# A decoder layer whose gates and branches swap the stationary and the moving operand, and whose second FFN sums its norm two units later

## The chip, the cores and the metric

One core of one Trainium2 chip runs the whole layer in one launch. The metric is the device time of the launch in microseconds (us); the median of three runs of the kernel before is 2172.03 us (2171.75 to 2172.18).

## What is computed

The layer works on T = 272 tokens (16 meta tokens, which the output drops, and 256 others) of width 2048, in float32:

```
h += 1/2 * SwiGLU_1(RMSNorm(h))
u  = RMSNorm(h);  z = u @ W_in      # q, k, v, q_idx, k_idx, w_idx, x_c, B, C, gate_attn, gate_conv
y_A = sparse attention over the top 64 keys
y_B = B * conv3_causal(C * x_c)
merged = sigmoid(gate_conv) * (y_B @ W_conv_branch) + sigmoid(gate_attn) * (y_A @ W_attn_branch)
h += merged @ W_out
h += 1/2 * SwiGLU_2(RMSNorm(h))
```

The change lies in the lines of `merged`, in the order of `merged @ W_out`, and at the start of SwiGLU_2. Gates have 2048 rows of weights, branches 1024 each, `W_out` 2048; all three have 2048 columns.

## The kernel before, in words

**Products.** Each float32 operand is split into a high and a low float32r part, and a product is the sum of three: high times high, high times low, low times high. Weights come from memory in chunks of 1 MB (128 x 2048), issued by SP (L94). A chunk is split in two *units* of 128 x 1024: ScalarE copies the high part (`whi`, L109), VectorE subtracts it (`wlo`, L110). `Stream.next` hands out the blocks of a unit one after the other. When it begins a unit it issues, in this order: what is due `early`, one of the `steps`, the split of the unit that is three units ahead (AHEAD = 3, four buffers), and then what is due `later`. A function filed with lag n, once a product's last unit has been taken, is issued with the n-th unit that begins from then on. Each engine keeps that order, so that what is due `later` stands behind the split on VectorE and ScalarE.

**Three forms of product.** `mac` (L265 to L267, used by `fmajor`) holds a weight block of 128 x 128 and moves the activations, 272 columns at a time, three matmuls a block. `paired` (L279, L280) also holds the weight block, and moves the high and the low part of 256 tokens side by side: one matmul of 512 columns with `whi`, one of 256 with `wlo`; its result has two halves, which `joined` or `add_to` sums (ScalarE copies one half, VectorE adds the other). `tokens` (L290 to L292) holds 128 tokens of the activations and moves 512 columns of weights, three matmuls for each of two blocks of tokens (j = 1, 2); its result has tokens on the partitions.

**Around the change.** The gates and branches are `paired`, for one of 16 blocks of 128 features at a time: 16 steps of k for the gate `pgt`, 8 for the branch `pbr`, first for all 16 blocks of the convolution, then for all 16 of the attention. `gate` (L937) joins, multiplies by the row `R` of the norm and a Sigmoid follows on ScalarE (L973); `conv_merge` and `attn_merge` join and multiply, and the latter adds the two branches and splits the sum into `ms`, which has features on the partitions as `W_out` needs it. Then 16 `paired` products `po` give the new h (`add_to`), and for each block `next_act` and `square` prepare the second FFN. That FFN (`ffn_tokens`, L448) uses `tokens`; `turn_s` turns its product back with 32 x 32 transposes on VectorE (L446), four for each r. At its start the two halves of the sum of squares are added (L472, lag 2), TensorE sums over partitions (`across`, L467, early, lag 3), and `root` and `inverse` make the column `rcol` (lags 3 and 4), by which the first `gate` scales eight units after the start. 32 transposes of h (`turn_h`) are issued one a unit from the fifth unit on.

Of the kernel before, what the change touches and what calls it, by code (L numbers as in the profile page):

```python
# [15 lines left out]
P = 128  # L16
# [139 lines left out]
def tile_decoder_layer(  # L156
# [32 lines left out]
    def chunks(src, i0, i1, width=P):  # L189
        for i in range(i0, i1):  # L190
            st.add(src[i], RAW // width, width)
# [8 lines left out]
    chunks(wqi, 0, 8, 512)  # L200
    chunks(wq, 0, 8, 512)
    chunks(wcv, 0, 3 * KC)
    chunks(wgc, 0, KD * 3 // 2)
    chunks(wga, 0, KD * 3 // 2)
    chunks(wo, 0, KD)
    gu = down = 0
    for n in GROUPS:
# [61 lines left out]
    def fmajor(ps, xhi, xlo, n):  # L269

        for k in range(n):
            whi, wlo = st.next()
            mac(ps, whi, wlo, xhi(k), xlo(k), k == 0, k == n - 1)

    def paired(ps, x, n):

        for k in range(n):
            whi, wlo = st.next()
            nc.tensor.matmul(ps.rearrange("p (a t) -> p a t", a=2), whi, x(k), start=k == 0, stop=False)  # L279
            nc.tensor.matmul(ps[:, :SEQ], wlo, x(k)[:, 0, :], start=False, stop=k == n - 1)  # L280

    def tokens(ps_of, x, n):

# [160 lines left out]
    def turned(dst, src, rows, cols):  # L444

        nc.vector.transpose(dst[rows * 32 : rows * 32 + 32], src[cols * 32 : cols * 32 + 32])  # L446

    def ffn_tokens():  # L448

        with tc.tile_pool(name="ffn2", bufs=1, reuse_waits="tile") as fp:  # L450
            ht = fp.tile([P, 2, D], F32, name="ht")
            mid = fp.tile([P, 4 * GROUPS[0], 2, SEQ], F32R, name="mid")

            def turn_h(j, q, r):
                to = ht[:, j].rearrange("p (f b) -> p f b", b=P)
                at = META + j * P + q * 32
                turned(to[:, :, r * 32 : r * 32 + 32], h[:, :, at : at + 32], q, r)

            st.steps.extend([lambda: None] * 4)
            st.steps.extend(lambda j=j, q=q, r=r: turn_h(j, q, r) for j in range(2) for q in range(4) for r in range(4))  # L460

            ps = aux_tile("norm")

            def across():
                for j in (1, 2):
                    t0 = TT[j][0]
                    nc.tensor.matmul(  # L467
                        ps[:, 0, 2 * j : 2 * j + 2], ssq[0][:, t0 : t0 + P], ones[:, :2], start=True, stop=True
                    )

            root, inverse = rsqrt(rcol[:, 2:6], ps[:, 0, 2:6], (P, 4), 1.0 / D)
            st.later(lambda: nc.vector.tensor_add(ssq[0][:, META:], ssq[0][:, META:], ssq[1][:, META:]), 2)  # L472
            st.early(across, 3)
            st.later(root, 3)
            st.later(inverse, 4)

            def gate(pg, s):
                for j in (1, 2):
                    nc.scalar.activation(s[:, j - 1], pg[j], AF.Silu, scale=rcol[:, 2 * j : 2 * j + 1])

            def times(pu, s):
                for j in (1, 2):
                    nc.vector.scalar_tensor_tensor(
                        s[:, j - 1], pu[j], rcol[:, 2 * j : 2 * j + 1], s[:, j - 1], op0=ALU.mult, op1=ALU.mult
                    )

            def turn_s(mt, s, r):
                for q in range(4):
                    turned(
                        mt.rearrange("p f (j r b) -> p r j f b", j=2, r=4)[:, r],  # L490
                        s.rearrange("p j (f q b) -> p q j f b", f=4, q=4)[:, q],
                        q, r,
                    )

            def add(d, j, pd, last):
                to = ht[:, j - 1, d * 512 : (d + 1) * 512]
                nc.vector.scalar_tensor_tensor(to, pd, 0.5, to, op0=ALU.mult, op1=ALU.add)
                if last:
                    queue = nc.gpsimd if st.n_loaded < len(st.loads) else (nc.sync, nc.scalar)[j - 1]
                    queue.dma_start(out[j - 1, :, d * 512 : (d + 1) * 512], to)  # L500

            for c, n in enumerate(GROUPS):
                for f in range(n):
                    s = fp.tile([P, 2, 512], F32, name="s", bufs=2)
                    mt = fp.tile([P, 4, SEQ], F32, name="mt", bufs=2)
                    pg = {j: mm_tile(f"pg{j}") for j in (1, 2)}
                    tokens(pg, act_tokens, KD)
                    st.later(lambda pg=pg, s=s: gate(pg, s))
                    pu = {j: mm_tile(f"pu{j}") for j in (1, 2)}
                    tokens(pu, act_tokens, KD)  # L510
                    st.later(lambda pu=pu, s=s: times(pu, s))
                    for r in range(4):
                        st.later(lambda mt=mt, s=s, r=r: turn_s(mt, s, r), 2 + r)
                    to = mid[:, 4 * f : 4 * f + 4]
                    st.later(lambda to=to, mt=mt: split_into(to[:, :, 0], to[:, :, 1], mt), 6)
                for d in range(D // 512):
                    pd = {j: mm_tile(f"pd{j}") for j in (1, 2)}
                    tokens(pd, lambda k, j, part: mid[:, k, part, (j - 1) * P : j * P], 4 * n)
                    for j in (1, 2):
                        st.later(lambda d=d, j=j, ps=pd[j], c=c: add(d, j, ps, c == 1))  # L520
            st.flush()
# [16 lines left out]
    with ExitStack() as mix:  # L538
# [6 lines left out]
        qT = mp.tile([P, H, SEQ], F32, name="qT", tag="tB")  # L545
        ys = mp.tile([P, H, 2, SEQ], F32R, name="ys")
        cs = [mp.tile([P, KC // 2, 2, SEQ], F32R, name=f"cs{i}", tag=f"c{i}") for i in range(2)]
        vt = [mp.tile([P, G * HD], F32, name=f"vt{j}") for j in range(3)]
        kT = mp.tile([P, G, T], F32, name="kT")
        kiT = mp.tile([P, T], F32, name="kiT")  # L550
        acc = [mp.tile([P, T], F32, name=f"acc{j}") for j in range(2)]
        zk = [mp.tile([P, G * HD + NKW], F32, name=f"zk{j}") for j in range(3)]

        steps = st.steps
# [376 lines left out]
            st.flush()  # L931


        m = [mp.tile([P, 8, SEQ], F32, name=f"m{i}", tag=t) for i, t in enumerate(("tA", "tB"))]
        ms = {}

        def gate(pgt):  # L937
            sg = mw.tile([P, SEQ], F32, name="sg", tag="cy")
            joined(sg, pgt)
            nc.vector.tensor_mul(sg, sg, R[:, META:])  # L940
            return sg

        def conv_merge(d, pcb, sg):
            to = m[d // 8][:, d % 8, :]
            joined(to, pcb)
            nc.vector.tensor_mul(to, to, sg)

        places = [("c0", 4), ("c1", 4), ("zz0", 2), ("zz1", 2), ("tA", 4)]

        def attn_merge(d, pab, sg):  # L950
            t = mw.tile([P, SEQ], F32, name="t", tag="cy")
            joined(t, pab)
            nc.vector.tensor_mul(sg, t, sg)
            nc.vector.tensor_add(sg, sg, m[d // 8][:, d % 8, :])
            if d not in ms:
                tag, n = places.pop(0)
                t = mp.tile([P, n, 2, SEQ], F32R, name=f"ms{d}", tag=tag)
                ms.update({d + i: t[:, i] for i in range(n)})
            split_into(ms[d][:, 0, :], ms[d][:, 1, :], sg)

        def conv_out(k):
            return cs[k // 4][:, k % 4]

        def attn_out(k):
            return ys[:, k]

        for branch, merge in ((conv_out, conv_merge), (attn_out, attn_merge)):
            for d in range(KD):
                box = {}
                pgt, pbr = mm_tile("pgt"), mm_tile("pbr")  # L970
                paired(pgt, narrow, KD)
                st.later(lambda pgt=pgt, box=box: box.update(s=gate(pgt)))
                st.later(lambda box=box: nc.scalar.activation(box["s"], box["s"], AF.Sigmoid), 2)  # L973
                paired(pbr, branch, KC)
                st.later(lambda d=d, pbr=pbr, box=box, merge=merge: merge(d, pbr, box["s"]))

        for d in range(KD):
            po = mm_tile("po")
            paired(po, lambda k: ms[k], KD)
            st.later(lambda d=d, po=po: add_to(h[:, d, META:], po, 1.0, True))  # L980
            st.later(lambda d=d: (next_act(d, gains[2], META, LATER), square(d, META)), 2)


    ffn_tokens()
# [21 lines left out]
    return np.ascontiguousarray(np.stack([_tiles(a, P), _tiles(b, P)], 1)).reshape(-1, P, KD * P)  # L1006


def _first(wgu):

    wgu[:4] = wgu[:4].reshape(4, P, KD, P).transpose(1, 2, 0, 3).reshape(P, 4, -1).transpose(1, 0, 2)
    return wgu


def _down(w):
# [6 lines left out]


def _branch(gate, w):
    return _chunks(np.concatenate([_tiles(gate, P), _tiles(w, P)], 2))


def _columns(g):
# [22 lines left out]
def _layout(x, meta_tokens, ffn1_norm_g, ffn1_w_gate, ffn1_w_up, ffn1_w_down, mix_norm_g, w_in, q_norm_g,  # L1051
# [27 lines left out]
    a["wqi"], a["wq"] = _chunks(_tiles(qi, 512)), _chunks(_tiles(q, 512))  # L1079
    a["wcv"] = np.stack([_tiles(xc, P), _tiles(gc_, P), _tiles(gb, P)], 1).reshape(3 * KC, P, KD * P)  # L1080
    a["wgc"], a["wga"] = _branch(gcv, w_conv_branch[0]), _branch(ga, w_attn_branch[0])
    a["wo"] = _tiles(w_out[0], P)
    gu = np.stack([_tiles(ffn2_w_gate[0], 512), _tiles(ffn2_w_up[0], 512)], 1)
    a["wgu2"] = _chunks(gu.reshape(-1, P, KD * 512))
    a["wd2"] = _down_columns(ffn2_w_down[0])
# [20 lines left out]
```

## Time and profile before

| what | value |
|---|---|
| median of three runs | 2172.03 us (2171.75 to 2172.18) |
| the profiled execution, its own time | 2172.45 us |
| span of its trace | 2170.7 us |
| TensorE busy | 2160.4 us |
| VectorE busy | 1324.3 us |
| ScalarE busy | 979.4 us |
| granted TensorE clock, mean, as a share of 2.4 GHz | 1.00 |

The span is that of the instructions in the trace; the time of the execution is 1.75 us longer. A matmul's row gives its start and its whole length through a pipeline, so that successive rows overlap: the price of a matmul in a stream is the distance between starts, not its length. On VectorE and ScalarE rows of one engine overlap by at most about 0.1 us. In the timeline a bracket behind a row gives the time in which the engine stood idle before it, and who released it.

### The profile page before, as it was taken

How to read it: one execution, taken by the hardware profiler on the slowest of the kernel's cores; microseconds unless marked ns; L12 is line 12 of the kernel's file. 1: busy time of each engine (PE TensorE's matmuls, PEld its weight loads, DVE VectorE, ACT ScalarE, POOL GpSimd, SP SyncE). 2: the span in 40 equal slices, each digit the busy share in tenths (PEclk: the TensorE clock that was granted, in tenths of full speed). 3: DMA queues.
4: the chain of work that ended last, by engine and by line, in shares of the span. 5: the costliest groups of instructions: out<-in, count | busy, mean ns of one | idle time of the engine just before them, and what ended most of it. 6: DMA issues, size and time to landing. Idle time of an engine off the chain costs nothing.

```text
span 2170.7 us, 32296 instructions
## 1 busy us (share of the span) xinstructions
PE 2160.4 (100%) x13478; PEld 1955.1 (90%) x13478; DVE 1324.3 (61%) x1778; ACT 979.4 (45%) x1286; POOL 11.1 (1%) x18
## 2 busy tenths in 40 slices
PE   9999999999999999999999999999999999999999
PEld 9999999999999998798988888888888888888887
DVE  7555544455555555786566677668767644566664
ACT  6444433344444445564454455554444433444442
POOL 0000000000000000000000000000000000000000
PEclk9999999999999999999999999999999999999999
DMA  6555555555554545444455555555655555555564
GB/s 244 197 181 183 180 175 175 177 179 184 180 175 175 178 159 188 167 146 146 170 182 192 181 188 181 189 185 177 210 193 188 198 193 194 192 195 193 194 204 143
DMA packets 56626, 397.72 MB, mean 183 GB/s; under 512 B 6432, under 2 KB 7072, under 8 KB 8992
## 3 DMA queue, kind: packets, MB, share of 16 engines
q1 hardware_dynamic: 55584, 393.95, 52.9%
q8 instruction: 105, 1.72, 0.3%
q0 software_dynamic: 320, 1.05, 0.1%
q10 hardware_dynamic: 576, 0.67, 0.1%
q14 instruction: 41, 0.34, 0.0%
HBM read 393.54 MB, written 2.10 MB: 182 GB/s over the span
## 4 chain that ended last, share of the span: by engine, by line
PE 96%; DVE 2%; ACT 1%; DMA 1%; issue 0%; ACTq 0%; DVEq 0%
PE pgt L279 6%; PE pd L265 4%; PE pd L267 4%; PE pd L266 4%; PE pu L267 4%; PE pu L266 4%; PE pu L265 4%; PE pg L267 4%; PE pg L266 4%; PE pg L265 4%; PE pu L292 4%; PE pd L290 4%; PE pd L291 4%; PE pu L291 4%; PE pu L290 4%; PE pd L292 4%
## 5 line engine op out<-in xcount | busy, mean ns | idle before, releaser
L110 DVE TENSOR_TENSOR wlo<-raw,whi 128x1024 fp32r<-128x1024 f32 (+1 forms) x747 | 913.0, 1222 | 788.1 <-ACT whi L109 785.5
L109 ACT ACTIVATE whi<-raw 128x1024 fp32r<-128x1024 f32 (+1 forms) x747 | 788.8, 1057 | 1040.1 <-PE pd L266 144.3
L265 PE MATMUL pd<-mid,whi 128*128 128x272 f32 x704 | 201.7, 287 | 0.0
L266 PE MATMUL pd<-mid,whi 128*128 128x272 f32 x704 | 201.7, 287 | 0.0
L267 PE MATMUL pd<-mid,wlo 128*128 128x272 f32 x704 | 201.7, 287 | 0.0
L265 PE MATMUL pg<-act,whi 128*128 128x272 f32 x672 | 192.7, 287 | 0.0
L267 PE MATMUL pg<-act,wlo 128*128 128x272 f32 x672 | 192.5, 287 | 0.0
L267 PE MATMUL pu<-act,wlo 128*128 128x272 f32 x672 | 192.5, 287 | 0.0
L266 PE MATMUL pg<-act,whi 128*128 128x272 f32 x672 | 192.5, 287 | 0.0
L265 PE MATMUL pu<-act,whi 128*128 128x272 f32 x672 | 192.5, 287 | 0.0
L266 PE MATMUL pu<-act,whi 128*128 128x272 f32 x672 | 192.5, 287 | 0.0
L279 PE MATMUL pgt<-act,whi 128*128 128x512 f32 x512 | 182.2, 398 | 0.0
L280 PE MATMUL pgt<-act,wlo 128*128 128x256 f32 x512 | 143.8, 281 | 0.0
L290 PE MATMUL pg<-whi,act 128*128 128x512 f32 x352 | 137.1, 389 | 0.0
L291 PE MATMUL pg<-wlo,act 128*128 128x512 f32 x352 | 136.9, 389 | 0.0
L292 PE MATMUL pg<-whi,act 128*128 128x512 f32 x352 | 136.9, 389 | 0.0
L290 PE MATMUL pu<-whi,act 128*128 128x512 f32 x352 | 136.9, 389 | 0.0
L290 PE MATMUL pd<-whi,mid 128*128 128x512 f32 x352 | 136.9, 389 | 0.0
L292 PE MATMUL pd<-whi,mid 128*128 128x512 f32 x352 | 136.9, 389 | 0.0
L292 PE MATMUL pu<-whi,act 128*128 128x512 f32 x352 | 136.9, 389 | 0.0
L291 PE MATMUL pu<-wlo,act 128*128 128x512 f32 x352 | 136.9, 389 | 0.0
L291 PE MATMUL pd<-wlo,mid 128*128 128x512 f32 x352 | 136.9, 389 | 0.0
(224 smaller groups left out, 4168.2 us busy)
## 6 DMA issues: line engine op xcount, KB each, us to landing
raw<-in_wgu_dram SPq DMA_DIRECT2D x175, 1024.0 KB, 4.9
raw<-in_wd_dram SPq DMA_DIRECT2D x88, 1024.0 KB, 4.9
raw<-in_wcv_dram SPq DMA_DIRECT2D x24, 1024.0 KB, 4.9
raw<-in_wgc_dram SPq DMA_DIRECT2D x24, 1024.0 KB, 4.8
raw<-in_wga_dram SPq DMA_DIRECT2D x24, 1024.0 KB, 4.8
raw<-in_wo_dram SPq DMA_DIRECT2D x16, 1024.0 KB, 4.8
raw<-in_wqi_dram SPq DMA_DIRECT2D x8, 1024.0 KB, 4.8
raw<-in_wq_dram SPq DMA_DIRECT2D x8, 1024.0 KB, 4.8
```

What stands on the lines that cost most here:

```text
L109: nc.scalar.activation(hi[:, :n], raw, AF.Copy)
L110: nc.vector.tensor_sub(lo[:, :n], raw, hi[:, :n].bitcast(F32))
L265: nc.tensor.matmul(ps, whi, xhi, start=first, stop=False)
L266: nc.tensor.matmul(ps, whi, xlo, start=False, stop=False)
L267: nc.tensor.matmul(ps, wlo, xhi, start=False, stop=last)
L279: nc.tensor.matmul(ps.rearrange("p (a t) -> p a t", a=2), whi, x(k), start=k == 0, stop=False)
L280: nc.tensor.matmul(ps[:, :SEQ], wlo, x(k)[:, 0, :], start=False, stop=k == n - 1)
L290: nc.tensor.matmul(ps, xhi, whi, start=k + i == 0, stop=False)
L291: nc.tensor.matmul(ps, xhi, wlo, start=False, stop=False)
L292: nc.tensor.matmul(ps, xlo, whi, start=False, stop=k + i == n - 1)
```

## The change

Gates and branches take the form `tokens`, for four groups of 512 features in place of 16 blocks of 128. The Sigmoid reads the product where it lies, scaled by `rcol`, one instruction for each j; the merges are two multiplications of 128 x 512, and for the attention an addition of 128 x 1024. The sum then has tokens on the partitions: it is turned by 16 transposes a group (`turn_columns`, which is `turn_s` moved) and split by `to_ms` in one piece a group, for the last group in half as many units. The first four blocks of `W_out` are computed side by side, k outermost, so that the last rows of `ms` are needed later; their weights are stored in that order. Some tiles are joined so that their room can be used again. The sum for the norm of the second FFN, and what follows from it, are filed two units later.

```diff
-    chunks(wgc, 0, KD * 3 // 2)
-    chunks(wga, 0, KD * 3 // 2)
+    chunks(wgc, 0, KD * 3 // 2, 512)
+    chunks(wga, 0, KD * 3 // 2, 512)
...
+    def pair(ps, whi, wlo, x, first, last):
+        nc.tensor.matmul(ps.rearrange("p (a t) -> p a t", a=2), whi, x, start=first, stop=False)
+        nc.tensor.matmul(ps[:, :SEQ], wlo, x[:, 0, :], start=False, stop=last)
...
+    def turn_columns(mt, s, r):
+
+        for q in range(4):
+            turned(
+                mt.rearrange("p f (j r b) -> p r j f b", j=2, r=4)[:, r],
+                s.rearrange("p j (f q b) -> p q j f b", f=4, q=4)[:, q],
+                q, r,
+            )
...
-            st.later(lambda: nc.vector.tensor_add(ssq[0][:, META:], ssq[0][:, META:], ssq[1][:, META:]), 2)
-            st.early(across, 3)
-            st.later(root, 3)
-            st.later(inverse, 4)
+            st.later(lambda: nc.vector.tensor_add(ssq[0][:, META:], ssq[0][:, META:], ssq[1][:, META:]), 3)
+            st.early(across, 5)
+            st.later(root, 5)
+            st.later(inverse, 6)
...
         def gate(pgt):
-            sg = mw.tile([P, SEQ], F32, name="sg", tag="cy")
-            joined(sg, pgt)
-            nc.vector.tensor_mul(sg, sg, R[:, META:])
+            sg = mp.tile([P, 2, 512], F32, name="sg", tag="vts")
+            for j in (1, 2):
+                nc.scalar.activation(sg[:, j - 1], pgt[j], AF.Sigmoid, scale=rcol[:, 2 * j : 2 * j + 1])
             return sg
...
+        def conv_merge(g, pbr, sg):
+            for j in (1, 2):
+                nc.vector.tensor_mul(m[g // 2][:, g % 2, j - 1], pbr[j], sg[:, j - 1])
+
+        places = [("c0",), ("c1",), ("zz0", "zz1"), ("tA",)]
+
+        def attn_merge(g, pbr, sg):
+            for j in (1, 2):
+                nc.vector.tensor_mul(sg[:, j - 1], pbr[j], sg[:, j - 1])
+            nc.vector.tensor_add(sg, sg, m[g // 2][:, g % 2])
+            mt = mp.tile([P, 4, SEQ], F32, name="mt", tag="keys")
+            per = 2 if g == 3 else 1
+            for r in range(4):
+                st.later(lambda r=r: turn_columns(mt, sg, r), 2 + r // per)
+            st.later(lambda: to_ms(g, mt), 2 + 4 // per)
+
+        def to_ms(g, mt):
+            tags = places[g]
+            n = 4 // len(tags)
+            for i, tag in enumerate(tags):
+                t = mp.tile([P, n, 2, SEQ], F32R, name=f"ms{4 * g + n * i}", tag=tag)
+                split_into(t[:, :, 0], t[:, :, 1], mt[:, n * i : n * (i + 1)])
+                ms.update({4 * g + n * i + k: t[:, k] for k in range(n)})
...
         for branch, merge in ((conv_out, conv_merge), (attn_out, attn_merge)):
-            for d in range(KD):
+            for g in range(4):
                 box = {}
-                pgt, pbr = mm_tile("pgt"), mm_tile("pbr")
-                paired(pgt, narrow, KD)
+                pgt = {j: mm_tile(f"pgt{j}") for j in (1, 2)}
+                tokens(pgt, act_tokens, KD)
                 st.later(lambda pgt=pgt, box=box: box.update(s=gate(pgt)))
-                st.later(lambda box=box: nc.scalar.activation(box["s"], box["s"], AF.Sigmoid), 2)
-                paired(pbr, branch, KC)
-                st.later(lambda d=d, pbr=pbr, box=box, merge=merge: merge(d, pbr, box["s"]))
-
+                pbr = {j: mm_tile(f"pbr{j}") for j in (1, 2)}
+                tokens(pbr, branch, KC)
+                st.later(lambda g=g, pbr=pbr, box=box, merge=merge: merge(g, pbr, box["s"]))
+
+
+        two = [aux_tile(f"po{i}") for i in range(2)]
+        four = [two[i // 2][:, i % 2] for i in range(4)]
+        for k in range(KD):
+            for ps in four:
+                whi, wlo = st.next()
+                pair(ps, whi, wlo, ms[k], k == 0, k == KD - 1)
         for d in range(KD):
-            po = mm_tile("po")
-            paired(po, lambda k: ms[k], KD)
-            st.later(lambda d=d, po=po: add_to(h[:, d, META:], po, 1.0, True))
-            st.later(lambda d=d: (next_act(d, gains[2], META, LATER), square(d, META)), 2)
+            if d < 4:
+                po, lag = four[d], 1 + d // 2
+            else:
+                po, lag = mm_tile("po"), 1
+                paired(po, lambda k: ms[k], KD)
+            st.later(lambda d=d, po=po: add_to(h[:, d, META:], po, 1.0, True), lag)
+            st.later(lambda d=d: (next_act(d, gains[2], META, LATER), square(d, META)), lag + 1)
...
-    return _chunks(np.concatenate([_tiles(gate, P), _tiles(w, P)], 2))
+    return _chunks(np.concatenate([_tiles(gate, 512), _tiles(w, 512)], 2))
...
-    a["wo"] = _tiles(w_out[0], P)
+    a["wo"] = _first(_tiles(w_out[0], P))
```

## Rows read from the trace of the kernel before

**Rows 1.** Page: busy time by engine, and the engines' shares of the final chain.

```profile
PE 2160.4 (100%) x13478; PEld 1955.1 (90%) x13478; DVE 1324.3 (61%) x1778; ACT 979.4 (45%) x1286; POOL 11.1 (1%) x18
...
PE 96%; DVE 2%; ACT 1%; DMA 1%; issue 0%; ACTq 0%; DVEq 0%
```

**Rows 2.** Waits of TensorE: what it waited for, total us, times, longest.

```profile
PE norm L467 <- DVE ssq L472: 1.0, 1, 1.0
```

**Rows 3.** Timeline of TensorE, first gate, first `po`, first matmuls of the second FFN.

```profile
1085.03 0.40 PE L279 MATMUL pgt<-act,whi 128*128 128x512 f32 x1
1085.26 0.28 PE L280 MATMUL pgt<-act,wlo 128*128 128x256 f32 x1
...
1356.39 0.40 PE L279 MATMUL po<-ms,whi 128*128 128x512 f32 x1
...
1446.84 0.40 PE L290 MATMUL pg<-whi,act 128*128 128x512 f32 x1
```

**Rows 4.** Timeline of TensorE, second FFN: second group's first matmul, and the last.

```profile
1492.16 0.39 PE L290 MATMUL pg<-whi,act 128*128 128x512 f32 x1
...
2166.49 0.39 PE L292 MATMUL pd<-whi,mid 128*128 128x512 f32 x1
```

**Rows 5.** Timeline of TensorE, one paired product of the convolution, first and next.

```profile
1045.33 0.40 PE L279 MATMUL pb<-act,whi 128*128 128x512 f32 x1
...
1050.88 0.28 PE L265 MATMUL pxc<-act,whi 128*128 128x258 f32 x1
```

**Rows 6.** Timeline of TensorE, the norm sum inside the second FFN's first product.

```profile
1452.12 0.39 PE L292 MATMUL pg<-whi,act 128*128 128x512 f32 x1
1453.50 0.61 PE L467 MATMUL norm<-ones,ssq 128*128 128x2 f32 x4 [0.99 <-DVE ssq L472]
1453.97 0.48 PE L290 MATMUL pg<-whi,act 128*128 128x512 f32 x1
```

**Rows 7.** Timeline of TensorE, six such small matmuls that wait for nothing.

```profile
797.84 0.73 PE L371 MATMUL norm<-ones,ssq 128*128 128x2 f32 x6
798.43 0.37 PE L265 MATMUL pkv<-act,whi 128*128 128x272 f32 x1
```

**Rows 8.** Windows, gate stage and a second-FFN stretch: PE, PEld, DVE, ACT, POOL, clock, DMA.

```profile
1085.00:1356.30 271.30, 271.30 (x1538) 235.39 (x1537) 179.50 (x255) 134.76 (x208) 0.74 (x1) 1.00 0.54 185
...
1500.00:1700.00 200.00, 200.00 (x884) 165.65 (x883) 146.20 (x181) 88.70 (x89) 0.00 (x0) 1.00 0.57 195
```

**Rows 9.** Groups of VectorE by form: count, busy us, mean ns, idle before.

```profile
L446 DVE STREAM_TRANSPOSE mt<-s 32x256 f32<-32x256 f32 x176 | 76.7, 436 | 2.8
L446 DVE STREAM_TRANSPOSE ht<-h 32x512 f32<-32x512 f32 x32 | 22.5, 703 | 0.9
L483 DVE SCALAR_TENSOR_TENSOR s<-pu,rcol,s 128x512 f32<-128x512 f32 x22 | 15.4, 742 | 0.0
L568 DVE TENSOR_TENSOR zz<-zz,small 128x1024 f32<-128x1024 f32 x2 | 2.4, 1220 | 0.2 <-ACT zz L567 0.2
```

**Rows 10.** Groups of ScalarE by form: count, busy us, mean ns, idle before.

```profile
L479 ACT ACTIVATE s<-pg,rcol 128x512 f32<-128x512 f32 x22 | 13.8, 676 | 0.0
```

**Rows 11.** Timeline of VectorE, second FFN: turning and splitting one group.

```profile
1592.30 1.22 DVE L110 TENSOR_TENSOR wlo<-raw,whi 128x1024 fp32r<-128x1024 f32 x1
1593.55 1.80 DVE L446 STREAM_TRANSPOSE mt<-s 32x256 f32<-32x256 f32 x4
1595.38 1.23 DVE L110 TENSOR_TENSOR wlo<-raw,whi 128x1024 fp32r<-128x1024 f32 x1
1596.53 1.22 DVE L315 TENSOR_TENSOR mid<-mt,mid 128x1024 fp32r<-128x1024 f32 x1
```

**Rows 12.** Timeline of ScalarE, end of the first `po`.

```profile
1362.12 1.06 ACT L109 ACTIVATE whi<-raw 128x1024 fp32r<-128x1024 f32 x1 [0.68 <-PE po L279]
1364.87 0.38 ACT L310 ACTIVATE u<-po 128x256 f32<-128x256 f32 x1 [1.68 <-DVE h L307]
```

**Rows 13.** Timeline of VectorE, the same stretch.

```profile
1363.21 1.23 DVE L110 TENSOR_TENSOR wlo<-raw,whi 128x1024 fp32r<-128x1024 f32 x1 [0.51 <-ACT whi L109]
1364.36 0.41 DVE L307 SCALAR_TENSOR_TENSOR h<-po,h 128x256 f32<-128x256 f32 x1
```

More of the change, by code (lines that the diff above doesn't have):

```diff
@@ L278, in paired @@
             whi, wlo = st.next()
-            nc.tensor.matmul(ps.rearrange("p (a t) -> p a t", a=2), whi, x(k), start=k == 0, stop=False)
-            nc.tensor.matmul(ps[:, :SEQ], wlo, x(k)[:, 0, :], start=False, stop=k == n - 1)
+            pair(ps, whi, wlo, x(k), k == 0, k == n - 1)
     def tokens(ps_of, x, n):
@@ L484, in times @@
                         s[:, j - 1], pu[j], rcol[:, 2 * j : 2 * j + 1], s[:, j - 1], op0=ALU.mult, op1=ALU.mult
[L485 to L492, printed above, removed]
                     )
@@ L512, in ffn_tokens @@
                     for r in range(4):
-                        st.later(lambda mt=mt, s=s, r=r: turn_s(mt, s, r), 2 + r)
+                        st.later(lambda mt=mt, s=s, r=r: turn_columns(mt, s, r), 2 + r)
                     to = mid[:, 4 * f : 4 * f + 4]
@@ L547, in tile_decoder_layer @@
         cs = [mp.tile([P, KC // 2, 2, SEQ], F32R, name=f"cs{i}", tag=f"c{i}") for i in range(2)]
[L548 to L551, printed above, removed]
+        vts = mp.tile([P, 4, G * HD], F32, name="vts", tag="vts")
+        vt = [vts[:, j] for j in range(3)]
+        keys = mp.tile([P, 4, T], F32, name="keys", tag="keys")
+        kT, kiT = keys[:, :G], keys[:, G]
+        acc = [keys[:, G + 1], mp.tile([P, T], F32, name="acc1")]
         zk = [mp.tile([P, G * HD + NKW], F32, name=f"zk{j}") for j in range(3)]
@@ L931, in tile_decoder_layer @@
             st.flush()
-        m = [mp.tile([P, 8, SEQ], F32, name=f"m{i}", tag=t) for i, t in enumerate(("tA", "tB"))]
+        m = [mp.tile([P, 2, 2, 512], F32, name=f"m{i}", tag=t) for i, t in enumerate(("tA", "tB"))]
         ms = {}
         def gate(pgt):
-            sg = mw.tile([P, SEQ], F32, name="sg", tag="cy")
-            joined(sg, pgt)
-            nc.vector.tensor_mul(sg, sg, R[:, META:])
-            return sg
[L943 to L965, printed above, removed]
+            sg = mp.tile([P, 2, 512], F32, name="sg", tag="vts")
+            for j in (1, 2):
+                nc.scalar.activation(sg[:, j - 1], pgt[j], AF.Sigmoid, scale=rcol[:, 2 * j : 2 * j + 1])
+            return sg
+        def conv_merge(g, pbr, sg):
+            for j in (1, 2):
+                nc.vector.tensor_mul(m[g // 2][:, g % 2, j - 1], pbr[j], sg[:, j - 1])
@@ new lines, in to_ms, with conv_out, attn_out @@
+        def to_ms(g, mt):
[5 more added lines that the diff above has]
+                ms.update({4 * g + n * i + k: t[:, k] for k in range(n)})
+        def conv_out(k, j, part):
+            return cs[k // 4][:, k % 4, part, (j - 1) * P : j * P]
+        def attn_out(k, j, part):
+            return ys[:, k, part, (j - 1) * P : j * P]
@@ L1006, in _pairs, with _first @@
     return np.ascontiguousarray(np.stack([_tiles(a, P), _tiles(b, P)], 1)).reshape(-1, P, KD * P)
-def _first(wgu):
-    wgu[:4] = wgu[:4].reshape(4, P, KD, P).transpose(1, 2, 0, 3).reshape(P, 4, -1).transpose(1, 0, 2)
-    return wgu
+def _first(tiles):
+    tiles[:4] = tiles[:4].reshape(4, P, KD, P).transpose(1, 2, 0, 3).reshape(P, 4, -1).transpose(1, 0, 2)
+    return tiles
 def _down(w):
```

## The prediction
> **What bounds the kernel now.** I read the page first. TensorE is busy for 2160.4 of 2170.7 us and has 96% of the chain that ended last [rows 1]. A busy TensorE can still be one that waits inside its stream, so the waits came next: the longest wait of TensorE behind another engine is 1.0 us in the whole list, and it stands at the norm sum that this change moves [rows 2]. None lies in the gate stage. There the time is therefore the price of a matmul in its stream times their number, and I took both from starts in the timeline. The gate stage runs from 1085.03 to 1356.39 us, 271.36 us, and the products with `W_out` from there to 1446.84, 90.45 us [rows 3]; the windows show no idle TensorE in it at a granted clock of 1.00, the 2.4 GHz level [rows 8]. VectorE is busy for 179.5 of its 271.3 us and ScalarE for 134.8: neither bounds it, but both feed TensorE with split weights, so what counts is whether a unit's `wlo` comes in time.
>
> **The change, part by part.** *Form of the gates and branches.* Before: 2 branches x 16 blocks x 24 steps of k are 768 pairs (512 + 256 columns), so a pair costs 271.36 / 768 = 353.3 ns; the 256 pairs of `W_out` give 90.45 / 256 = 353.3 ns again [rows 3]. After: 2 x 4 groups x 24 steps x 6 matmuls are 1152 matmuls of 512 columns. Their price is that of the second FFN. It has 11 x 192 matmuls for gate and up and 1056 for down, 3168; behind its first group (192) stand 2976, and from the first to the last start pass 2166.49 - 1492.16 = 674.33 us [rows 4]; over 2975 distances that is 226.7 ns. So 1152 x 226.7 ns = 261.1 us in place of 271.4: **10.2 us less**. Four pairs (1413 ns) and the six matmuls that take their place (1360 ns) stream the same 3072 columns; the gain is 53 ns for each of 192 steps. What the price can be elsewhere: at most two thirds of a pair, 235.5 ns (then nothing is gained); below 226.7 no row of a steady stream goes. I take 226.7, because those matmuls have the same three operands in the same order, with the same splits and turns running beside them. That a pair's price is not wholly fixed shows in one product of the convolution: 16 pairs in 5.55 us, 346.9 ns [rows 5]. If the reordered `W_out` fell to that, its 256 pairs would save 1.6 us more; I take 0 and keep 1.6 for the range.
>
> *The norm sum.* Between 1452.12 and 1453.97 one matmul of 227 ns and four small ones passed [rows 6], so the sum costs 1.85 - 0.23 = 1.62 us of stream. Six small ones without a wait take 0.59 us [rows 7], so four take about 0.4: 1.2 us go, with the bracket's 0.99 as the lower bound; I take **1.1 us less**. That the wait does go: a unit of this form lasts 12 x 0.227 = 2.72 us. The addition is now issued with the third unit, 5.4 us after the start, behind whi and wlo (2.3 us) [rows 12, 13], and takes about 0.4: done near 8.1, asked for at the fifth unit, 10.9. What moves along with it (four matmuls, root with its table load, the small operations of the inverse; no DMA, so no queue of SP or POOL is passed) comes behind two more splits and, for `root`, behind the first `turn_h` of 0.70 us [rows 9]. Its only reader is the first FFN gate, due with the ninth unit at 21.8 us; the inverse is issued with the sixth at 13.6. No cost.
>
> *VectorE and ScalarE in the gate stage.* An attention group has 12 wlo of 1.23 us, 2 products of 128 x 512 (nearest row 0.74), an addition of 1.22 [rows 9], 16 turns (four take 1.83 us from start to next start) and a split of 1.22 [rows 11]: about 26 us of the group's 12 x 2.72 = 32.6. A convolution group has 16.2. Four of each make 169 us, against 179.5 before. ScalarE's two Sigmoids a group, 0.68 us each by the nearest row [rows 10], replace joins and Sigmoids of smaller pieces. So the sum fits, and only bursts can hurt. Cover: a unit's wlo is done 2.3 us after it begins [rows 12, 13] and is used three units, 8.2 us, after: 5.9 us to spare. The merge puts VectorE 1.1 us late (1.1 + 1.15 + 1.5 + 1.1 against 3.8), four units with turns add 0.3 each, the next one recovers: 2.4 us late at worst. It costs **nothing**; without that cover it would cost those 2.4 us a group. The second FFN does this eleven times at an even 226.7 ns [rows 4, 11]. SP's loads are as many and as large; the stage is 4% shorter, 185 GB/s would become 192, less than the 195 that the second FFN draws [rows 8].
>
> *The start of `W_out`.* This place is tight. A unit of eight pairs lasts 2.83 us, and the unit that needs the last group's `ms` (k = 12) begins 17.0 us after the stage. VectorE's queue by the same rows: wlo from 1.1 us, two products to 3.6, addition to 4.75, wlo, eight turns to 9.6, wlo, eight turns to 14.45, wlo, split from 15.6 to 16.85. It arrives with the need; I take **0.2 us more**, between 0 and a unit of 2.83. Then four products end together. In `add_to` ScalarE waits for VectorE on the same product (1.68 us of idle before `u`, released by `h`) [rows 12, 13], so the two take turns, and the next whi stands behind. Followed through in the same way, the wlo of the seventh unit from there is done at 17.0 us and used at 17.1: I take **0.1 us more**, between 0 and 2.
>
> Sum: -10.2 - 1.1 + 0.3 = **-11.0 us**. It is made against the profiled execution, 2172.45 us (span 2170.7 and 1.75 around it), which gives 2161.45; the median is 0.42 lower, so **2161.0 us**.
>
> **Rivals.** *A: the price lies in the columns, not in the form.* If what a column costs in this stage (353.3 / 768 = 0.460 ns) held for either form, 1152 x 512 columns would again take 271.3 us, and only the norm's 1.1 us would go: 2170.9 us. For it: the columns are equal in number, and one paired product ran at 346.9 ns in the same form [rows 5]. Against it: the second FFN starts with the very next matmul after `W_out` and settles at 0.443 ns a column. The Trainium skill ("TensorE: Matmul & The Clock Gate", section "Back-to-back issue gap") has such a rule: columns over 2.4 GHz plus 2.5 ns for each matmul when warm. By that rule two matmuls fewer in eight would save 5 ns a step, an estimate of 1.0 us in all and with the norm 2169.9 us; the trace disagrees with its figures for either form, since it shows 353.3 and 226.7 ns where the rule gives 325 and 216. Chance 0.06.
>
> *B: `W_out` waits for the turned sum.* The start of `W_out` goes late by one unit, because the turns, the split or the hand-overs between ScalarE and VectorE take longer than the second FFN's rows say: 2161.0 + 2.83 = 2163.8 us. For it: no spare time at all. Against it: every duration there is a measured one. Chance 0.10.
>
> *C: the turns hold the splits up, and the kernel is slower.* The place is VectorE's queue in the four attention groups. A turn writes and reads 32 partitions with strides in another tile than before; if it took 0.95 us instead of 0.46, a group would be 2.4 + 7.8 = 10.2 us late, 4.3 beyond the 5.9 to spare, and at W_out's start 7.8 late: 3 x 4.3 + 7.8 - 11.0 = 9.7 us over, 2181.7 us. The gain of 11.0 us is eaten up from about 0.79 us a turn (3 x (16 x 0.33 - 3.5) + 16 x 0.33 = 11). Against it: the same function takes 0.44 us in 176 cases, and a turn of twice the width 0.70 [rows 9]. Chance 0.03.
>
> That the change does not do what it says could only be at the norm: if it still waited, 1.1 us would stay, 2162.1 us, inside the range.
>
> **The numbers.** 0.2% of the time is 4.3 us, about what a measurement of this kernel can tell from no change. The forecast has 0.81 and rival B 0.10; both are faster by more than that: 0.91. Rival A is within it: 0.06. Rival C is slower: 0.03. The range starts 1.6 us (W_out at 346.9 ns) and some rounding below the forecast, at 2159.0, and ends at 2164.2 behind rival B; it leaves out A, C, and the case in which both tight places cost more than a unit together.
>
> **What would show it right or wrong.** Right: in the timeline the first gate matmul and the first `po` stand 261 us apart, starts in between at 0.227 us; no wait of TensorE in the list behind `wlo` or `ms`; the bracket at the norm gone; 64 turns of 0.44 us more on VectorE. Wrong: starts at 0.235 us (A); a wait of TensorE on `ms` at the seventh unit of `W_out` (B); waits on `wlo` in attention groups (C).

## The result and the profile after

The changed kernel takes 2159.86 us (median of four runs, 2159.29 to 2160.8) against 2171.98; the ratio is 0.9944 with a 95% interval of 0.9932 to 0.9957. Run again, it took 2159.29 us (five runs, 2158.91 to 2159.78), ratio 0.9942 (0.9928 to 0.9955). The forecast was 2161.0 us with a range of 2159.0 to 2164.2. The profiled execution took 2159.29 us with a span of 2157.5, against 2170.7 before.

The page of the changed kernel, its lines on busy time and on the chain:

```profile
PE 2148.9 (100%) x13094; PEld 1936.0 (90%) x13094; DVE 1306.7 (61%) x1707; ACT 959.6 (44%) x1195; POOL 11.1 (1%) x18
...
PE 97%; DVE 1%; ACT 1%; DMA 1%; issue 0%; DVEq 0%
```

TensorE still bounds the kernel [rows 1]: it has 384 matmuls fewer and is busy for 11.5 us less. Where the time went is read from starts in the timeline of TensorE: the first gate matmul, the first product of `W_out`, the first matmul of the second FFN and the last of all.

```profile
1084.67 0.40 PE L293 MATMUL pgt<-whi,act 128*128 128x512 f32 x1
...
1345.82 0.39 PE L276 MATMUL po<-ms,whi 128*128 128x512 f32 x1
...
1434.96 0.39 PE L293 MATMUL pg<-whi,act 128*128 128x512 f32 x1
...
2153.31 0.39 PE L295 MATMUL pd<-whi,mid 128*128 128x512 f32 x1
```

| stretch | before [rows 3, 4] | after | difference |
|---|---|---|---|
| start to first gate | 1085.03 | 1084.67 | -0.36 |
| gates and branches | 271.36 | 261.15 | -10.21 |
| `W_out` | 90.45 | 89.14 | -1.31 |
| second FFN, first to last matmul | 719.65 | 718.35 | -1.30 |
| last matmul to the end | 4.21 | 4.19 | -0.02 |

The first line is no work of the change: this stretch differs by as much between executions of unaltered code (1084.50 with the norm alone changed, below). It leaves 12.8 us for the other lines; the medians of the first measurement differ by 12.1, those of the second by 12.7.

In the windows the gate stage (first row) and `W_out` (second row), with the columns of rows 8:

```profile
1084.60:1345.80 261.20, 261.20 (x1154) 216.30 (x1153) 154.77 (x170) 115.92 (x119) 0.74 (x1) 1.00 0.57 193
1345.80:1435.00 89.20, 89.20 (x514) 78.30 (x513) 69.73 (x109) 48.85 (x78) 0.00 (x0) 1.00 0.56 191
```

VectorE is busy for 154.8 us of the gate stage in place of 179.5, though it now turns (the 169 us of the forecast also held the last group's products, turns and split, some 11 us, which fall into `W_out`); the loads rise from 185 to 193 GB/s and TensorE never idles. The new operations, in the groups of VectorE and then ScalarE by form:

```profile
L449 DVE STREAM_TRANSPOSE mt<-sg 32x256 f32<-32x256 f32 x64 | 27.9, 436 | 1.0
...
L957 DVE TENSOR_TENSOR sg<-pbr,sg 128x512 f32<-128x512 f32 x8 | 5.1, 681 | 0.0
L958 DVE TENSOR_TENSOR sg<-sg,m 128x1024 f32<-128x1024 f32 x4 | 4.9, 1225 | 0.1
```

```profile
L946 ACT ACTIVATE sg<-pgt,rcol 128x512 f32<-128x512 f32 x16 | 10.0, 675 | 0.0
```

A turn costs what it cost in the second FFN, 436 ns [rows 9]; the product of 128 x 512 takes 681 ns where 742 was used, the Sigmoid 675 where 676 was.

### The profile page after: what moved, and what is told of

Its sections match the earlier page's. It is cut to its first block, busy times and chain, and to the rows that moved or that the text cites. A ratio compares the mean times of both kernels' runs of the same rounds, so it can differ in the third digit from the quotient of the medians.

```text
span 2157.5 us, 31256 instructions
## 1 busy us (share of the span) xinstructions
PE 2148.9 (100%) x13094; PEld 1936.0 (90%) x13094; DVE 1306.7 (61%) x1707; ACT 959.6 (44%) x1195; POOL 11.1 (1%) x18
## 4 chain that ended last, share of the span: by engine, by line
PE 97%; DVE 1%; ACT 1%; DMA 1%; issue 0%; DVEq 0%
PE pd L266 4%; PE pd L267 4%; PE pd L265 4%; PE pu L265 4%; PE pu L266 4%; PE pu L267 4%; PE pg L265 4%; PE pg L266 4%; PE pg L267 4%; PE pg L293 4%; PE pd L295 4%; PE pu L293 4%; PE pg L294 4%; PE pu L295 4%; PE pu L294 4%; PE pg L295 4%
## 5 line engine op out<-in xcount | busy, mean ns | idle before, releaser
L265 PEld LDWEIGHTS pd<-mid,whi 128*128 128x128 f32 x704 | 132.6, 188 | 0.0
L266 PEld LDWEIGHTS pd<-mid,whi 128*128 128x128 f32 x704 | 132.6, 188 | 0.0
```

The lines of the kernel that those rows point to most:

```text
L265: nc.tensor.matmul(ps, whi, xhi, start=first, stop=False)
L266: nc.tensor.matmul(ps, whi, xlo, start=False, stop=False)
```

## The experiments

Times stand beside runs of the kernel before on the same chip (2171.9 to 2172.0 us). Where no ratio is given, a kernel ran once. A "wait" below is a row of the list of TensorE's waits; a "stretch" is a distance between starts in its timeline.

**The norm sum undone, and done alone.** The changed kernel with the lags of before, and the kernel before with the new ones:

```diff
-            st.later(lambda: nc.vector.tensor_add(ssq[0][:, META:], ssq[0][:, META:], ssq[1][:, META:]), 3)
-            st.early(across, 5)
-            st.later(root, 5)
-            st.later(inverse, 6)
+            st.later(lambda: nc.vector.tensor_add(ssq[0][:, META:], ssq[0][:, META:], ssq[1][:, META:]), 2)
+            st.early(across, 3)
+            st.later(root, 3)
+            st.later(inverse, 4)
```

> The changed kernel with the norm sum of the second FFN filed as before. Theory (the norm's own wait was worth 1.2 to 1.3 us): the wait of TensorE on the sum, about 1.0 us, is back, the stretch around the four small matmuls takes about 1.85 us from the last gate matmul to the next, and the span is 1.2 us over the changed kernel's 2157.5, near 2158.8. Rival (the FFN's start gained for another reason, from the new order of W_out): the stretch from the FFN's first to its last matmul stays at 718.4 us.

> The kernel before with the later norm sum alone. Theory: 1.2 us under the span of before (2170.7), near 2169.5, all of it at the start of the second FFN; gate stage 271.3 us and W_out 90.45 us as before. Rival: no gain, because the FFN's first stretch waits elsewhere: 2170.7.

The timeline of TensorE with the sum as before in the changed kernel, and then as changed:

```profile
1440.15 0.39 PE L295 MATMUL pg<-whi,act 128*128 128x512 f32 x1
1441.55 0.61 PE L479 MATMUL norm<-ones,ssq 128*128 128x2 f32 x4 [1.02 <-DVE ssq L484]
1442.02 0.48 PE L293 MATMUL pg<-whi,act 128*128 128x512 f32 x1
```

```profile
1445.66 0.39 PE L295 MATMUL pg<-whi,act 128*128 128x512 f32 x1
1445.88 0.50 PE L479 MATMUL norm<-ones,ssq 128*128 128x2 f32 x4
1446.25 0.48 PE L293 MATMUL pg<-whi,act 128*128 128x512 f32 x1
```

From the matmul ahead of the sum to the one behind it pass 1.87 us and 0.59 us. The FFN's stretch is 719.64 us with the old lags (span 2158.7) and 718.37 with the new ones alone (span 2168.9, of which half a microsecond is an earlier first gate): 1.3 us either way, whatever the form of the gates. The two parts of the change add up.

**The order of `W_out` undone.** The 16 products one after the other, with what is due issued first:

```diff
-        for k in range(KD):
-            for ps in four:
-                whi, wlo = st.next()
-                pair(ps, whi, wlo, ms[k], k == 0, k == KD - 1)
+        st.flush()
         for d in range(KD):
-            if d < 4:
-                po, lag = four[d], 1 + d // 2
-            else:
-                po, lag = mm_tile("po"), 1
-                paired(po, lambda k: ms[k], KD)
+            po, lag = mm_tile("po"), 1
+            paired(po, lambda k: ms[k], KD)
...
-    a["wo"] = _first(_tiles(w_out[0], P))
+    a["wo"] = _tiles(w_out[0], P)
```

> The changed kernel with the 16 products of W_out one after the other, in the old order of weights, and everything that is due issued before the first of them. Theory (the last group's turns and split, 12.5 us of VectorE and ScalarE work behind the last branch, lie open where W_out does not begin with rows that are ready): TensorE waits on ms in the first product, which wants k = 12 after 4.2 us, for about 8 us: 2168 us. Rival (the four weight units ahead and the short turns hide it anyway): 2160 us.

It took 2169.68 us (2168.1 to 2170.89, ratio to before 0.9989, 0.9980 to 0.9999). The waits of TensorE begin with

```profile
PE po L276 <- DVE ms L318: 7.5, 1, 7.5
```

so the chain of turns and split does lie open when nothing else can be multiplied meanwhile. The stretch of `W_out` grew by 10.5 us to 99.63: 7.6 of wait, and the rest in what followed it, a lower clock and pairs at the price of before (1.4 us, below). In the windows around the wait the column behind POOL's count is the granted clock:

```profile
1349.00:1357.00 8.00, 1.12 (x7) 0.70 (x5) 6.70 (x15) 1.77 (x2) 0.00 (x0) 0.81 0.00 0
...
1358.00:1360.00 2.00, 2.00 (x7) 1.72 (x7) 1.81 (x2) 0.18 (x1) 0.00 (x0) 0.50 0.31 41
1360.00:1361.00 1.00, 1.00 (x5) 0.81 (x5) 0.00 (x0) 0.59 (x1) 0.00 (x0) 0.57 0.65 188
1361.00:1362.00 1.00, 1.00 (x8) 0.86 (x7) 0.50 (x1) 0.47 (x1) 0.00 (x0) 1.00 1.04 442
```

The clock stood at 0.50, the level of 1.2 GHz, for some 3 us of work behind the wait, which costs about 1.6 us. The new order of `W_out` is therefore not a detail: without it the change makes the kernel 0.1% faster, with it 0.6%.

**The last group turned like the others**, four turns a unit:

```diff
-            per = 2 if g == 3 else 1
+            per = 1
```

> The changed kernel with the last group turned like the others, four turns a unit in place of eight, and split two units later. Theory (the chain of VectorE to the last ms ends just when it is needed): the split ends 19.5 us after the start of W_out, TensorE waits at k = 12 for about 2.6 us, span near 2160.0. Rival (there was room at that place): span 2157.5 as in the changed kernel.

VectorE's timeline ends the split at 1364.89, 19.4 us after the first product of `W_out` at 1345.50, and TensorE's shows who waits for it:

```profile
1363.67 1.22 DVE L318 TENSOR_TENSOR ms<-mt,ms 128x1024 fp32r<-128x1024 f32 x1
```

```profile
1362.33 0.28 PE L277 MATMUL po<-ms,wlo 128*128 128x256 f32 x1
1364.94 0.51 PE L276 MATMUL po<-ms,whi 128*128 128x512 f32 x1 [2.33 <-DVE ms L318]
```

The stream lost 2.61 us less a matmul's usual 0.12, as worked out; the run took 2162.84 us with a span of 2161.1, where 2160.0 was expected. The stretch of `W_out` is 93.04 us, 3.9 longer than in the changed kernel: 2.5 of it the wait, the other 1.4 the pairs behind it, which ran at the price of before (below).

**Every turn twice** in the gate stage:

```diff
-                st.later(lambda r=r: turn_columns(mt, sg, r), 2 + r // per)
+                st.later(lambda r=r: [turn_columns(mt, sg, r) for _ in range(2)], 2 + r // per)
```

> The changed kernel with each turn of the gate stage done twice, with the same result. Theory (5.9 us of cover, of which 2.4 are used): each of the first three attention groups is 2.4 + 7.3 = 9.7 us late, 3.8 beyond its cover, and the last ms is 7.3 us late: 3 x 3.8 + 7.3 = 18.7 us more, 2178.5 us. Rival 1 (only VectorE's sum counts, 26 + 7.3 us against 32.6 a group): about 0.7 us a group and 7.3 at W_out, 2169 us. Rival 2 (TensorE is never reached): 2160 us.

It took 2184.02 us (2182.36 to 2184.58), slower than before: ratio 1.0053 (1.0036 to 1.0070). The first waits of TensorE:

```profile
PE po L276 <- DVE ms L318: 7.0, 1, 7.0
PE pbr L294 <- DVE wlo L110: 6.0, 3, 2.0
PE pgt L294 <- DVE wlo L110: 4.8, 3, 1.6
```

Two waits on `wlo` in each of three groups stretch the stream by 3.9 us a group (1.76 and 2.16, distances of starts less the usual 0.227), where 3.8 was worked out from the cover, and the last `ms` is 7.0 us late, where 7.3 was. Both rivals fall: neither the sum of VectorE's work nor a TensorE that is out of reach gives these places. What the expectation lacked is 6.3 us (spans: 2182.5 - 2157.5 - 18.7), and the windows show most of it behind the waits, those of the first group to begin with:

```profile
1272.00:1274.00 2.00, 0.37 (x2) 0.31 (x3) 1.97 (x3) 1.65 (x2) 0.00 (x0) 0.98 0.34 143
1274.00:1276.00 2.00, 2.00 (x6) 1.62 (x5) 2.00 (x3) 2.00 (x3) 0.00 (x0) 0.50 0.00 0
1276.00:1278.00 2.00, 2.00 (x7) 1.54 (x7) 2.00 (x2) 1.40 (x3) 0.00 (x0) 0.66 0.59 115
1278.00:1280.00 2.00, 2.00 (x11) 1.61 (x10) 0.98 (x2) 1.06 (x1) 0.00 (x0) 1.00 1.00 414
```

TensorE is busy all the while, but at the lower clock. The third group shows the same; in the second, the same two waits, with the same work between them, left the clock at 1.00:

```profile
1310.00:1312.00 2.00, 0.09 (x1) 0.00 (x0) 1.94 (x4) 1.19 (x2) 0.00 (x0) 1.00 0.57 242
1312.00:1314.00 2.00, 1.91 (x8) 1.61 (x9) 2.00 (x3) 2.00 (x3) 0.00 (x0) 1.00 0.00 0
1314.00:1316.00 2.00, 2.00 (x10) 1.65 (x10) 2.00 (x3) 2.00 (x4) 0.00 (x0) 1.00 0.39 57
```

The gate stage is 15.8 us longer in all, 11.8 of it waits. Of the other 4.0 the two stretches at the lower clock cost 1.6 each, and the first starts behind the six waits the remaining 0.8. Why the clock fell in two of three groups is not shown. `W_out` is 9.5 us longer, 7.1 of it the wait on `ms`, the rest nearly all at the lower clock behind it.

**The price of a pair.** `W_out` came out 1.3 us shorter than before, which the forecast had not in its sum. In the changed kernel the first 48 pairs run at the 353.3 ns of before, then the matmul that needs the late `ms` is disturbed by a few hundredths of a microsecond (a row of 0.47 in place of 0.40), and all 208 pairs behind it run at 346.7:

```profile
1362.41 0.40 PE L276 MATMUL po<-ms,whi 128*128 128x512 f32 x1
1362.65 0.28 PE L277 MATMUL po<-ms,wlo 128*128 128x256 f32 x1
1362.77 0.47 PE L276 MATMUL po<-ms,whi 128*128 128x512 f32 x1
1363.08 0.28 PE L277 MATMUL po<-ms,wlo 128*128 128x256 f32 x1
```

208 x 6.7 ns = 1.4 us. That suggested that a break in the stream sets the price, and a break can be made: one product of two columns whose result is not used, ahead of the gates of the kernel before and ahead of `W_out` in the changed one.

```diff
+        nc.tensor.matmul(aux_tile("bub")[:, 0, :2], ones, ones[:, :2], start=True, stop=True)
```

> The kernel before with one small matmul (two columns, result unused) between the convolution and the first gate; all else unchanged. Theory P (a pair's price of 353.3 or 346.7 ns is set by how the stream was entered, and a break in the stream sets it): all 1024 pairs of gates, branches and W_out run at 346.7 ns, 1024 x 6.7 ns = 6.8 us less, about 2165.2 us. Rival F (353.3 ns belongs to the place or the form, and the cheaper pairs at the end of the changed kernel come from the reordered W_out): 2172.0 us, plus about 0.2 for the break. If P holds only until something disturbs the stream, the time lies between.

> The changed kernel with the same small matmul between the last branch and the first W_out product. Theory P: W_out's pairs run at 346.7 ns from the first one on in place of from the 49th, 48 x 6.7 ns = 0.3 us less and about 0.2 us for the break: 2159.8 us, no measurable difference, but the pairs' starts show it. Rival F: the first 48 pairs stay at 353.3 ns.

Ahead of the gates it changed nothing: 2172.16 us, ratio 1.0001 (0.9992 to 1.0010), and the gate stage still lasts 271.44 us. Theory P is refuted for this place. Ahead of `W_out` in the changed kernel the pairs settle at 346.7 ns within three, as P has it (starts of three successive pairs; the matmul with `wlo` lies in between):

```profile
1346.65 0.39 PE L276 MATMUL po<-ms,whi 128*128 128x512 f32 x1
...
1347.00 0.39 PE L276 MATMUL po<-ms,whi 128*128 128x512 f32 x1
...
1347.35 0.39 PE L276 MATMUL po<-ms,whi 128*128 128x512 f32 x1
```

and the time, 2159.41 us, ratio 0.9943 (0.9930 to 0.9955), is that of the changed kernel: `W_out` is 0.14 us shorter, and the gate stage with the break 0.15 longer. One more kernel put a break ahead of each of the 80 products in the kernel before, through a function `small_break()` with the same matmul:

```diff
+                small_break()
                 paired(pgt, narrow, KD)
...
+                small_break()
                 paired(pbr, branch, KC)
...
             po = mm_tile("po")
+            small_break()
```

> The kernel before with one small matmul ahead of each of the 32 gate, 32 branch and 16 W_out products: 80 entries into a stream of pairs. Theory C (either price can follow a break, whatever the operands): among gates, branches and W_out alike some products run at 346.7 ns and others at 353.3. Theory O (the moving operand decides: act, cs and ys dear, ms cheap): gates and branches stay at 353.3 ns, W_out runs at 346.7 ns in all 16. The breaks cost about 0.1 us each, 8 us; by C some 3 of them come back, span near 2176; by O 1.7 come back.

Its span is 2188.0 us, so a break costs (2188.0 - 2170.7) / 80 = 0.22 us, twice what was expected, and all 80 products, those of `W_out` among them, run at 353.3 ns behind it. Theory C would have had some at the lower price, theory O all of `W_out`: neither came. Taken together, one break was followed by the low price and 81 by the high one. Nor do the waits settle it: behind the wait of 7.0 us in the kernel with doubled turns `W_out` runs at 346.7, behind those of 7.5 and 2.3 us above at the higher price. The kernel before has both prices too, in its convolution: the sixth of eight paired products is the one at 346.9 ns [rows 5], and the seventh takes 5.65 us, 353.1 ns a pair:

```profile
1062.31 0.39 PE L279 MATMUL pb<-act,whi 128*128 128x512 f32 x1
...
1067.96 0.28 PE L265 MATMUL pxc<-act,whi 128*128 128x258 f32 x1
```

In all eleven traces of this case the sixth is at the low price and the first, seventh and eighth at the high one, so that the price of a place repeats from execution to execution. What is shown is that a pair has two steady prices with the same operands and the same clock, and that the price can change where the stream is disturbed; what decides which one follows is open.

**The changed kernel again**, unaltered:

> The changed kernel, unaltered, for its spread and a second profile. Theory C (the price of W_out's pairs after the late ms falls out either way from execution to execution): times lie in 2159.2 to 2160.9 us, wider than the 0.4 us of the kernel before, and W_out's stretch is 89.1 us in a short execution and about 90.5 in a long one. Rival (the spread has another source): W_out's stretch is 89.1 us whatever the execution's time.

The second profile has the same stretches, `W_out` 89.14 us, with a time of 2159.29, and so has that with the norm sum undone, 89.15 us: nothing here speaks for theory C. The five runs lie within 0.9 us, as do the nine of the kernel before beside them (2171.62 to 2172.51). No long execution was profiled, so whether the 2160.8 us of the first four runs was one with dear pairs is not settled.

## Why the prediction was right

**The form of gates and branches** was the forecast's main term, 10.2 us, and measured 10.21: 1152 matmuls at 226.7 ns, the price read from the second FFN [rows 4], in the same clock and with no wait. The rule of the Trainium skill by which columns and a fixed 2.5 ns a matmul make the time ("TensorE: Matmul & The Clock Gate", section "Back-to-back issue gap") gave an estimate of 1.0 us for this step; the trace disagrees with it after the change as before it, with 226.7 ns where the rule gives 216. Rival A, by which a column's price belongs to the stage, is refuted by the same 261.15 us.

**The norm sum** was put at 1.1 us and is worth 1.3, shown by undoing it and by doing it alone, one execution each. The working gave 1.2 and the bracket of the wait 0.99, and the value taken lay between them; without the wait the four small matmuls take 0.37 us, so that the whole of 1.2 and a little more went.

**VectorE's bursts** were costed at nothing, and cost nothing. That what is left of the cover was read rightly, 5.9 us less the 2.4 used, is shown by the kernel with doubled turns, whose waits on `wlo` came in the attention groups and as long as it said; the two numbers apart are not tested. Rival C's mechanism is thus real and makes the kernel slower than before; it does not act here because a turn costs 436 ns. Its price was too low: behind the waits of two of the three groups, and behind the wait on `ms`, TensorE worked on at 1.2 GHz for 3 to 4 us. The Trainium skill says of the clock that activity releases the throttle and that idleness brings it back (same page, "Part 1: The HAM clock gate"); the windows with 0.50 agree, but behind the same waits of the second group the clock stayed at 1.00.

**The start of `W_out`** was worked out to 16.85 us for the last split against a need at 17.0. It ended at 1361.47 + 1.22 = 1362.69, 16.87 us after the first product:

```profile
1355.45 1.23 DVE L110 TENSOR_TENSOR wlo<-raw,whi 128x1024 fp32r<-128x1024 f32 x1
1356.71 3.59 DVE L449 STREAM_TRANSPOSE mt<-sg 32x256 f32<-32x256 f32 x8
1360.33 1.23 DVE L110 TENSOR_TENSOR wlo<-raw,whi 128x1024 fp32r<-128x1024 f32 x1
1361.47 1.22 DVE L318 TENSOR_TENSOR ms<-mt,ms 128x1024 fp32r<-128x1024 f32 x1
```

TensorE lost less than 0.1 us to it, and none at the second tight place, the four products that end together; rival B did not come to pass, and the variants with one unit more or with the old order show how near it was.

**The mis-sized term** is that of `W_out`. The forecast took 0.3 us more for its two tight places and nothing for the pairs, and kept the 1.6 us of cheaper pairs for the lower end of the range. Measured is 1.3 us less: 208 of the 256 pairs took the lower price, 1.4 us, and the tight places cost under 0.1. That, with 0.2 at the norm, is the whole of 1.8 us by which the stretches beat the sum of 11.0; in the medians, 1.1 us remain of it in the first measurement and 1.7 in the second. Why these pairs took the lower price stays open, so that this part of the gain is not explained.

## What to carry to other kernels

When TensorE never waits, price a change of form by the distance between starts of that very form elsewhere in the trace: equal columns are not equal time, here 1360 ns against 1413 for the same 3072. When work moves to the engine that also feeds TensorE, compare the burst with the lead of the feed, not the sum with the span, and look at the last group apart, where nothing else is left to multiply; reorder what follows so that the late rows are used late. Look at the granted clock behind every long wait: the waits of 3.9 us a group here cost 1.6 us more by it in two groups of three.

## What had not been expected

- A pair of a 512- and a 256-column matmul has two steady prices, 353.3 and 346.7 ns, in the same kernel, with the same operands, at a granted clock of 1.00. It can change at a small disturbance, here at the late `ms`; of 82 deliberate breaks one was followed by the low price. Where nothing ahead of it was altered, a place had the same price in every trace.
- TensorE worked at a granted clock of 0.50 for 3 to 4 us behind two waits of 1.6 and 2.0 us with 2.6 us of work between them, in two groups of three, and behind the waits of 7.0 and 7.5 us; in the other group, and behind the single wait of 2.3 us, the clock stayed at 1.00.
- A product of two columns, two rows of the trace, costs 0.22 us in the middle of a stream; two such at the norm, four rows, cost 0.37.
